# PEER's dense gates: one-hots in groups of two tokens instead of four, sixteen products at a time

## The chip, the cores and the metric

One core of a Trainium2 chip runs the whole program. Its engines work side by side and wait for one another through semaphores: TensorE (PE, matmuls; PEld, its weight loads), VectorE (DVE), ScalarE (ACT), GpSimd (POOL) and SyncE (SP, which issues most DMAs). The metric is the device time of one execution in microseconds; smaller is better.

## What is computed

The reference is two transformer layers one after the other, 512 tokens of 1024 channels: a hybrid layer with a mixture of 64 experts, then a mixer (attention and retention) with a PEER layer. The change is in PEER. Each token has 8 heads; each head finds the 16 best of 128 first and 128 second keys, and of their sums the 16 best, which name 16 of 128 x 128 = 16384 experts. An expert is one row of u and one of v:

```
    sc, ci = lax.top_k(cand, PEER_TOPK)
    eidx = (e1 * PEER_NKEYS + e2).reshape(T, PEER_HEADS * PEER_TOPK)
    gates = jax.nn.softmax(sc, axis=-1).reshape(T, PEER_HEADS * PEER_TOPK).astype(x.dtype)
    ...
        act = jax.nn.gelu(jnp.einsum('td,tkd->tk', xt, peer_u[it]), approximate=False)
        return jnp.einsum('tk,tkd->td', gt * act, peer_v[it])
```

## The kernel before

PEER handles 384 of the 512 tokens densely: all 16384 activations of each (products over u), times a dense table of gates that is zero but for the 128 picks of the token, and products over v. The last 128 tokens' picks are gathered row by row beside that.

**The turns over u.** `peer_u` runs 128 turns. In each, PE does 24 matmuls p_pu of 384 columns (eight k tiles, three passes of a float32 split into whi and wlo), ACT applies Gelu (pact, or a tile that stays on chip), and DVE makes the wlo of a later turn, after ACT's whi; every second turn SP loads 1 MB of u (raw, three tiles deep) and stores the activations (actd). Beside this DVE has a list `work` of steps with estimated costs, which are spread over 120 of the 128 turns (`PACE_U`): first the top-k steps, then the dense gates. After them in each turn stand the gathered picks (`peer_picks`, prow, line 1990). DVE's order is the order of the code; PE, ACT, POOL and SP are put into order by a scheduler that works with modelled times.

**The dense gates.** `peer_gates` (line 1943) makes the table of four tokens a call, 96 calls. The gate of (second key, first key) is a sum over the token's 128 picks, which lie on the partitions; so it is a matmul of two one-hot matrices [128 picks, 128 keys], one of them weighted by the gate. A gate is the sum of two float16, ghi and glo, so there are two matmuls for each token, 768 in all (lines 1961 and 1962, p_gt). The one-hots are built by DVE for eight tokens at once, at every second call: hot2 and hot1 by comparing iota4 with the keys' numbers e2T and e1T (line 1954), ghi and glo by multiplying hot1 (lines 1955 and 1956); four operations on [128, 2, 128, 4] float16, that is two groups with the four tokens of a group side by side for each key:

```
            four = lambda n: pk[n][:, 32 * c + 4 * j:32 * c + 4 * j + 8].rearrange("p (g t) -> p g t", t=4)[:, :, None, :].to_broadcast(
                [128, 2, 128, 4])
```

One token's matrix is therefore read with a step of 4 elements, as weights (hot2) and as moving columns (ghi, glo). The results of four tokens fill one PSUM bank p_gt (two of them), which ACT copies into gst (line 1963); after 32 tokens SP stores gst, 2 MB, to gd (line 1965). `peer_v` reads gd back when all is done.

Of the kernel before, what the change touches and what calls it, by code (L numbers as in the profile page):

```python
# [10 lines left out]
F32 = mybir.dt.float32  # L11
# [11 lines left out]
# steps of the retention's q and k per turn of the attention  # L23
ATTN_RATE = 2
EPS = 1e-6
# PEER: tokens on the dense path, tiles of their activations that stay on chip (some in x's place); the pace of the work beside the products
# over u, the turns between which the other tokens' picks are gathered, and how many gathers run ahead
ND, KEEP, KEEP_X, PACE_U = 384, 20, 8, 120
PICK_START, PICK_END, AHEAD = 8, 254, 4
# MoE: weight tiles beside those of the other phases  # L30
RAW2 = 6
X_LOAD = (3, 4, 5, 6)
# the experts before which the shared expert's steps are taken
SHARED, TURN, SHARED_DOWN = (12, 19, 26, 33), (37, 41), (45, 48, 51, 54)
# key tiles of the neighbourhood windows, in column-major tokens
# [3 lines left out]
# columns of the packed per-partition vectors: name -> (first column, count)  # L39
# [12 lines left out]
# rows that are spread over the partitions: name -> (first, count)  # L52
# [3 lines left out]
class K:  # L56
# [60 lines left out]
    def split_raw(self, t, n=2048, step=1024):  # L117
        """a list of (hi, lo) for each step columns of t"""
        out = []
        for o in range(0, n, step):  # L120
            m = min(step, n - o)
            hi = self.pair.tile([128, 1024], F32R, name="whi", tag="whi")
            lo = self.pair.tile([128, 1024], F32R, name="wlo", tag="wlo")
            self.split(hi[:, :m], lo[:, :m], t[:, o:o + m])
            out.append((hi, lo))
        return out

    def halves(self, load, n, ahead=2):
        """(hi, lo) of the n halves of the tiles load(i), split some turns before they are used"""
# [12 lines left out]
    def proj(self, out, w, act, nk, cols=slice(None), start=True, stop=True):  # L142
        """out[m, t] (+)= sum over k of w[k, m] act[k, t]; w holds nk tiles [128, 128]"""
# [5 lines left out]
    def rstd(self, pool, ps, src, nch, n, width, tag="mm", bufs=None):  # L149
        """[128, n] in PSUM: 1 / sqrt(mean over the channels of src^2 + eps), on every partition"""  # L150
        return self.rstd_end(pool, ps, self.rstd_sums(pool, ps, src, nch, n, tag, bufs), n, width, tag, bufs)
# [28 lines left out]
    def modulated(self, pool, src, rb, a, b, hi, lo, chunks, n):  # L180
        """(hi, lo) of src * a * rb + b by channel (a, b: columns)"""
# [7 lines left out]
    # ------------------------------------------------------------------ first block, up to the MoE  # L189
    def block1(self):  # L190
        nc, A = self.nc, self.A
        with ExitStack() as es:
# [4 lines left out]
            # the sums of the experts' results, in two parts, and 128 rows for the empty places  # L197
            self.yd = [d.tile([640, 1024], F32, name=f"yd{i}") for i in range(2)]
            self.dr = d = self.pool(es, "b1_dram", space=DRAM)
            # q, k of each head of the neighbourhood as [hi, lo, hi], [hi, hi, lo]: one product over them is the three  # L200
# [8 lines left out]
            # zeros, then the accumulator of the other modulation  # L209
# [29 lines left out]
    def mod_mix(self, ps, p, q, x):  # L239
        """the modulation's columns of sh_mix, sc_mix, for x and ctx; the latter as norm_mix_g (1 + sc). And the rstd of x."""  # L240
# [33 lines left out]
    def meta_norm(self, q):  # L274
        """the meta tokens' norm by g_mix"""
# [14 lines left out]
    def qkv(self, q, s, w, ctx, mod, hc):  # L290
# [22 lines left out]
        for g in range(7):  # L313
            if g:
                w = self.load_pair(A["w_qkv"][g])
            for j in range(2):
# [25 lines left out]
                elif t < 10:  # L342
                    if t == 8:
                        # there's time for it after this
# [14 lines left out]
        # v of the neighbourhood: tokens on partitions  # L359
# [12 lines left out]
    def tiny_qk(self, q, pt, pc, rope, perm):  # L372
# [5 lines left out]
        # the rotations' swapped halves, and k moved to the lower partitions  # L378
# [51 lines left out]
    def na(self):  # L430
        """the neighbourhood attention, four heads at a time, beside the products of the spatial gating's v"""
# [89 lines left out]
    def v_steps(self, q):  # L521
        """v, turned so that tokens are on partitions, in small steps"""
# [48 lines left out]
    def gating(self, es):  # L571
        """spatial gating: v mixed over the chunk, the tiny attention's output, times u"""
# [34 lines left out]
    def mod_rest(self, s):  # L607
        """the modulation's other columns (g_mix, sh_ffn, sc_ffn, g_ffn), a quarter in four steps:
        acc[d, i] += silu(c)[d] w_ada[d, i]; sc_ffn as norm_ffn_g (1 + sc)"""
# [69 lines left out]
    # ------------------------------------------------------------------ the MoE  # L679
    # Its input is (x a) rstd + b, by channels; products over x a need no rstd: it is a token's, and comes after them.  # L680
    def ffn_open(self):
# [3 lines left out]
        # the places, from 1 on, four times  # L685
# [9 lines left out]
        # a token's number + 1, its weight for an expert in three parts that add up to it  # L695
# [11 lines left out]
    def ffn_begin(self, q):  # L707
        """b and its products with the router, on every partition"""
# [3 lines left out]
        # x a, then the MoE's input, then x by tokens  # L712
# [22 lines left out]
    def row_of(self, out, m):  # L735
        """four columns of modf as a row, on every partition"""
# [4 lines left out]
    def ffn_chunk(self, S, m):  # L741
        """when 128 channels of x are final"""
# [7 lines left out]
        if m == 6:  # L750
            # the table of Sqrt is loaded ahead
# [72 lines left out]
    def route(self, q, S):  # L824
        """the tokens' rstd, the MoE input's rows in DRAM, from which the experts gather, and who gathers what"""
# [13 lines left out]
        # scores, the eight best, and their weights  # L839
# [23 lines left out]
        # a token's place in its expert's list, and the first two experts' tokens  # L863
# [6 lines left out]
        # places from 1 on, 0 for the tokens that aren't in the list  # L870
# [8 lines left out]
    def route_end(self):  # L879
        """the experts' weights, by token"""  # L880
# [13 lines left out]
    def parts(self, out, w, rest):  # L894
        """w as the sum of three fp16 in out's last dimension"""
# [6 lines left out]
    def hots(self, e, hots, out, cols):  # L902
        """out[i] = cols of the token at place i of expert e's list"""
# [4 lines left out]
    def slots(self, e0, n):  # L908
        """for n experts the tokens of their first 128 places, and their weights"""
# [16 lines left out]
    def blocks(self, q):  # L926
        """counts beyond 128: which expert each further block of 128 places belongs to, and its first place"""
# [15 lines left out]
        # experts all of whose further blocks come before block b  # L943
# [8 lines left out]
        # first place: 128 (1 + block - blocks of the experts before)  # L952
# [6 lines left out]
    def rows_of(self, q, v, g):  # L959
        """v: token + 1, or 0 in an empty place -> its row, or one beyond all tokens'"""  # L960
# [5 lines left out]
    def places(self, q, pt, g, w):  # L966
        """pt: (token + 1 or 0, its weight's parts) per place -> rows (of the last ones), weights"""
# [7 lines left out]
    def shared(self, step):  # L975
        """the shared expert's gates and ups, in four steps"""
# [12 lines left out]
    def by_tokens(self, m0):  # L989
        """512 channels of x, tokens on partitions"""  # L990
# [8 lines left out]
    def shared_down(self, step):  # L999
        """x += g_ffn * the shared expert, by tokens, in four steps"""  # L1000
# [19 lines left out]
    def expert_load(self, e):  # L1020
        """the weights of expert e (a number, or in a register): [gate | up] in two halves of its rows, down"""
# [17 lines left out]
    def expert_block(self, xg, gi, ws, w, yd):  # L1039
        """adds the rows' results times ws and g_ffn to yd; w: the expert's weights, or what loads them"""  # L1040
# [38 lines left out]
    def spare_places(self):  # L1079
        """the first block beyond an expert's first 128 places, if any"""  # L1080
# [11 lines left out]
    def overflow(self, n):  # L1092
        """the other such blocks, one at a time"""
# [14 lines left out]
    def further(self, c, gi, ws):  # L1108
        """the tokens, and their weights, of the 128 places of expert c[0] from place c[1] on"""
# [18 lines left out]
    def tail_loads(self):  # L1128
        """what the sum of the results and the next norm need"""
# [5 lines left out]
    def routed_first(self):  # L1135
        """the first accumulated results"""
# [11 lines left out]
    def load_after(self, src, x):  # L1148
        """src, loaded once x is there"""
# [5 lines left out]
    # ------------------------------------------------------------------ the second block's mixer  # L1155
    def mixer(self):
        with ExitStack() as es:
# [3 lines left out]
            # the tokens, then the meta tokens  # L1161
# [1090 lines left out]
```

## Time and profile before

| what | us |
|---|---|
| three runs, lowest, median, highest | 3225.7, 3234.66, 3238.91 |
| span of the profiled execution | 3229.2 |
| PE busy (share of the span) | 3114.6 (96%) |
| DVE busy | 2240.4 (69%) |
| ACT busy | 1390.3 (43%) |
| first product of the gates starts at | 2313.1 |
| last product of the gates starts at | 2644.3 |

The span runs from the first to the last instruction of the profiled execution; that execution's time is not listed apart from it, and the span lies within the times of the three runs. The gates' stretch is a tenth of the program. In the profile a line of a helper (102 for most matmuls, 105 and 106 for the split into whi and wlo) serves many tiles, so the tiles' names tell which product is meant; buffer numbers are left out, so hot stands for hot1 and hot2, and piota for iota4.

### The profile page before, as it was taken

What the parts mean: (1) busy time and instruction counts of PE and PEld (TensorE: products, weight loads), DVE (VectorE), ACT (ScalarE), POOL (GpSimd) and SP (SyncE); (2) the same over time, 40 slices, a digit from 0 to 9 for tenths busy, and PEclk for the clock granted to TensorE, in tenths of its full rate; (3) what the DMA queues carried; (4) which work ended last, traced back from release to release, by engine and by line L of the source; (5) the groups of instructions that cost most, each with busy time, mean ns of one, the idle gap of its engine ahead of it and who ended that gap; (6) DMA issues with size and microseconds to landing.
All of it is one profiled execution on the core that took longest, in us unless ns stands there. A gap on an engine that the chain in (4) does not pass through costs nothing.

```text
span 3229.2 us, 45060 instructions
## 1 busy us (share of the span) xinstructions
PE 3114.6 (96%) x16976; PEld 2613.2 (81%) x16976; DVE 2240.4 (69%) x4077; ACT 1390.3 (43%) x2195; POOL 567.2 (18%) x452
## 2 busy tenths in 40 slices
PE   8999999999999999799999999999999999999997
PEld 4877888666666666587877788999999999999997
DVE  7467744687767777657532336999977867888885
ACT  5356433454444544354454324444444433333332
POOL 0200000132223223200000000233422213222221
PEclk9999999899999999999999999999999999999999
DMA  6554645499999999831211223677888889999996
GB/s 245 173 173 137 229 152 205 145 371 324 355 332 334 359 355 346 260 134 66 77 68 50 80 97 119 222 272 272 274 311 287 296 288 335 348 342 347 344 343 195
DMA packets 236495, 779.99 MB, mean 242 GB/s; under 512 B 28773, under 2 KB 108133, under 8 KB 190453
## 3 DMA queue, kind: packets, MB, share of 16 engines
q1 hardware_dynamic: 167136, 570.88, 48.1%
q0 software_dynamic: 66368, 200.38, 20.7%
q10 hardware_dynamic: 2772, 5.85, 0.5%
q8 instruction: 134, 2.20, 0.3%
q14 instruction: 85, 0.69, 0.1%
HBM read 692.29 MB, written 101.97 MB: 246 GB/s over the span
## 4 chain that ended last, share of the span: by engine, by line
PE 80%; DVE 7%; issue 5%; DMA 4%; ACT 2%; POOL 0%; SPq 0%; POOLq 0%; DVEq 0%; ACTq 0%
PE p_y L102 16%; PE p_pu L102 11%; PE p_gu L102 10%; PE p_y L1072 6%; PE p_za L102 3%; PE p_ga L102 3%; PE p_z L102 2%; DVE wlo L106 2%; PE p_xt L1046 2%; PE p_all L1267 1%; PE p_gt L1961 1%; PE p_gt L1962 1%; PE p_rg L102 1%; PE p_out L102 1%; PE p_mx L102 1%
## 5 line engine op out<-in xcount | busy, mean ns | idle before, releaser
L105 ACT ACTIVATE whi<-raw 128x1024 fp32r<-128x1024 f32 (+1 forms) x686 | 711.4, 1049 | 1037.2 <-PE p_gu L102 241.4
L106 DVE TENSOR_TENSOR wlo<-raw,whi 128x1024 fp32r<-128x1024 f32 (+1 forms) x686 | 822.7, 1207 | 405.8 <-ACT whi L105 378.5
L102 PE MATMUL p_pu<-xp,whi 128*128 128x384 f32 x2048 | 533.6, 339 | 5.0 <-ACT pact L1836 4.8
L102 PEld LDWEIGHTS p_pu<-xp,whi 128*128 128x128 f32 x2048 | 370.0, 189 | 8.0 <-ACT pact L1836 7.6
L102 PE MATMUL p_gu<-whi,xt 128*128 128x512 f32 x1040 | 357.3, 412 | 0.2 <-ACT whi L105 0.2
L102 PE MATMUL p_pu<-xp,wlo 128*128 128x384 f32 x1024 | 347.8, 341 | 4.6 <-DVE wlo L106 4.4
L102 PE MATMUL p_y<-vlo,whi 128*128 128x384 f32 x1024 | 342.0, 334 | 0.0
L102 PE MATMUL p_y<-vhi,wlo 128*128 128x384 f32 x1024 | 342.0, 334 | 0.0
L102 PE MATMUL p_y<-vhi,whi 128*128 128x384 f32 x1024 | 287.7, 334 | 1.4 <-ACT pkept L1836 1.4
L1980 POOL DMA_INDIRECT prow<-in_pu_rows,rows x128 | 182.7, 1427 | 465.7 <-DVE prow L1990 425.5
L1072 PE MATMUL p_y<-raw,eat 128*128 128x512 f32 x520 | 236.4, 595 | 2.7 <-DVE eat L1066 1.5
L102 PEld LDWEIGHTS p_gu<-whi,xt 128*128 128x128 f32 x1040 | 197.5, 190 | 50.5 <-issue 11.2
L102 PE MATMUL p_gu<-wlo,xt 128*128 128x512 f32 x520 | 223.2, 429 | 4.9 <-DVE wlo L106 4.7
L1980 POOL DMA_INDIRECT prow<-in_pv_rows,rows x128 | 140.3, 1096 | 369.6 <-DVE yr L1996 356.4
L102 PEld LDWEIGHTS p_pu<-xp,wlo 128*128 128x128 f32 x1024 | 193.1, 189 | 10.0 <-DVE wlo L106 9.6
L102 PEld LDWEIGHTS p_y<-vhi,wlo 128*128 128x128 f32 x1024 | 192.2, 188 | 0.0
L102 PEld LDWEIGHTS p_y<-vlo,whi 128*128 128x128 f32 x1024 | 192.2, 188 | 0.0
L102 PEld LDWEIGHTS p_y<-vhi,whi 128*128 128x128 f32 x1024 | 187.3, 188 | 1.7 <-ACT pkept L1836 1.7
L1072 PEld LDWEIGHTS p_y<-raw,eat 128*128 128x128 f32 x520 | 97.5, 191 | 101.7 <-issue 89.6
L1076 POOL DMA_INDIRECT yd<-ey,gidx x64 | 116.2, 1816 | 282.5 <-DVE ey L1075 266.0
L1996 DVE SCALAR_TENSOR_TENSOR yr<-prow,pdots,yr 128x1024 f32<-128x1024 f32 x128 | 163.8, 1279 | 0.2
L1990 DVE SCALAR_TENSOR_TENSOR prow<-prow,xr 128x1024 f32<-128x1024 f32 x128 | 155.3, 1217 | 1.6 <-DMA prow<-in_pu_rows,rows 1.5
(704 smaller groups left out, 5658.0 us busy)
## 6 DMA issues: line engine op xcount, KB each, us to landing
raw<-in_w_moe SPq DMA_DIRECT2D x195, 1024.0 KB
raw<-in_pu SPq DMA_DIRECT2D x64, 1024.0 KB
raw<-in_pv_rows SPq DMA_DIRECT2D x64, 1024.0 KB
raw<-in_w_mod SPq DMA_DIRECT2D x24, 1024.0 KB
gd<-gst SPq DMA_DIRECT2D x12, 2048.0 KB
vgt<-gd SPq DMA_DIRECT2D x32, 768.0 KB
actd<-pact SPq DMA_DIRECT2D x54, 384.0 KB
vact<-actd SPq DMA_DIRECT2D x54, 384.0 KB
```

The costliest lines, as they stand in the source:

```text
L102: nc.tensor.matmul(out, a, b, start=start and i == 0, stop=stop and i == len(passes) - 1)
L105: self.nc.scalar.activation(hi, src, AF.Copy)
L106: (lo_engine or self.nc.vector).tensor_tensor(lo, src, hi.bitcast(F32), ALU.subtract)
L1046: nc.tensor.transpose(pt[:, 128 * k:128 * k + 128], xg[:, 512 * g + 128 * k:512 * g + 128 * k + 128], self.ident)
L1072: nc.tensor.matmul(py, at[:, 128 * k:128 * k + 128], wd[:, 1024 * k + 512 * n:1024 * k + 512 * n + 512], start=k == 0, stop=k == 1)
L1076: nc.gpsimd.indirect_dma_start(out=yd[:], out_offset=bass.IndirectOffsetOnAxis(ap=gi, axis=0), in_=y[:], in_offset=None, bounds_check=639, ...
L1267: self.nc.tensor.matmul(pts[i][:, :264], w[a][:, 128 * k:128 * k + 128], self.hn[b][:, k, 264 * i:264 * i + 264], start=k == 0 and n == 0, ...
L1961: nc.tensor.matmul(pt[:, i, :], hots["hot2"][:, j % 2, :, i], hots["ghi"][:, j % 2, :, i], start=True, stop=False)
L1962: nc.tensor.matmul(pt[:, i, :], hots["hot2"][:, j % 2, :, i], hots["glo"][:, j % 2, :, i], start=False, stop=True)
L1980: nc.gpsimd.indirect_dma_start(out=t[:], out_offset=None, in_=A["pu_rows" if i < 128 else "pv_rows"], in_offset=bass.IndirectOffsetOnAxis( ...
L1990: nc.vector.scalar_tensor_tensor(t, t, 1.0, self.xr, ALU.mult, ALU.mult, accum_out=dots[:, k:k + 1])
L1996: nc.vector.scalar_tensor_tensor(self.yr, t, dots[:, k:k + 1], self.yr, ALU.mult, ALU.add)
```

## The change

The one-hots are laid out [128, 4, 128, 2]: four groups of two tokens, so a token's matrix is read with a step of 2 elements; iota4 becomes iota2, half as long. A call of `peer_gates` now covers eight tokens (48 calls, at twice the estimated cost), builds the four one-hot tiles, and puts their sixteen matmuls, the two copies and, after the fourth call, the store of gst into a function. That function goes into `self.late` and runs in the next turn, after its p_pu and Gelu and ahead of that turn's steps for DVE. The opening of the pool for the products over v is put off in the same way.

```
-        self.iota4 = p.tile([128, 128, 4], F16, name="piota4")
+        self.iota2 = p.tile([128, 128, 2], F16, name="piota2")
...
         for c in range(ND // 32):
-            for j in range(8):
-                work.append((1.3, lambda c=c, j=j: self.peer_gates(self.pg, c, j)))
-        work.append((0.0, gates_done))
+            for j in range(4):
+                work.append((2.6, lambda c=c, j=j: self.peer_gates(self.pg, c, j)))
+        work.append((0.0, lambda: self.late.append(gates_done)))
...
                 nc.scalar.activation(act[:, j, :], pt[:, :ND], AF.Gelu)
+                late, self.late = self.late, []
+                for f in late:
+                    f()
                 while at < len(work) and done <= total * (2 * g + j + 1) / PACE_U:
...
-        if j % 2 == 0:
-            four = lambda n: pk[n][:, 32 * c + 4 * j:32 * c + 4 * j + 8].rearrange("p (g t) -> p g t", t=4)[:, :, None, :].to_broadcast(
-                [128, 2, 128, 4])
-            hots = {n: q.tile([128, 2, 128, 4], F16, name=n, tag=n) for n in ("hot2", "hot1", "ghi", "glo")}
...
+        two = lambda n: pk[n][:, 32 * c + 8 * j:32 * c + 8 * j + 8].rearrange("p (g t) -> p g t", t=2)[:, :, None, :].to_broadcast(
+            [128, 4, 128, 2])
+        hots = {n: q.tile([128, 4, 128, 2], F16, name=n, tag=n) for n in ("hot2", "hot1", "ghi", "glo")}
...
-        pt = ps.tile([128, 4, 128], F32, name="p_gt", tag="gt", bufs=2)
-        hots = self.gate_hots
-        for i in range(4):
-            nc.tensor.matmul(pt[:, i, :], hots["hot2"][:, j % 2, :, i], hots["ghi"][:, j % 2, :, i], start=True, stop=False)
-            nc.tensor.matmul(pt[:, i, :], hots["hot2"][:, j % 2, :, i], hots["glo"][:, j % 2, :, i], start=False, stop=True)
-        nc.scalar.activation(self.gst[:, :, 4 * j:4 * j + 4], pt.rearrange("p a b -> p b a"), AF.Copy, scale=2.0 ** -14)
-        if j == 7:
-            nc.sync.dma_start(self.gd[c], self.gst)
+        def products():
+            if j == 0:
+                self.gst = q.tile([128, 128, 32], F32, name="gst", tag="gst")
+            for o in (0, 4):
+                pt = ps.tile([128, 4, 128], F32, name="p_gt", tag="gt", bufs=2)
+                for i in range(4):
+                    g, t = divmod(o + i, 2)
+                    nc.tensor.matmul(pt[:, i, :], hots["hot2"][:, g, :, t], hots["ghi"][:, g, :, t], start=True, stop=False)
+                    nc.tensor.matmul(pt[:, i, :], hots["hot2"][:, g, :, t], hots["glo"][:, g, :, t], start=False, stop=True)
+                nc.scalar.activation(self.gst[:, :, 8 * j + o:8 * j + o + 4], pt.rearrange("p a b -> p b a"), AF.Copy, scale=2.0 ** -14)
+            if j == 3:
+                nc.sync.dma_start(self.gd[c], self.gst)
+        self.late.append(products)
```

On DVE the instructions stand in the same order as before. On PE the scheduler made other groups. First PE, in the middle of one block of eight tokens, near the middle of the gates' stretch, before: p_gt_22144 and p_gt_22189 are the PSUM tiles of its first and last four tokens, hot2_22136 its one-hots as weights, p_pu the products over u of the turn.

```order
L1961 LDWEIGHTS hot2_22136
L1961 MATMUL p_gt_22144<-ghi_22138,hot2_22136 128x128
L1962 LDWEIGHTS hot2_22136
L1962 MATMUL p_gt_22144<-glo_22139,hot2_22136 128x128
L102 MATMUL p_pu_22159<-xp0_16673,wlo_22041 128x384
L102 MATMUL p_pu_22159<-xp0_16673,whi_22040 128x384
L102 MATMUL p_pu_22159<-xp1_16674,whi_22040 128x384
L102 MATMUL p_pu_22159<-xp0_16673,wlo_22041 128x384
L1961 LDWEIGHTS hot2_22136
L1961 MATMUL p_gt_22189<-ghi_22138,hot2_22136 128x128
```

And at the same block now (lines 1971 and 1972 are the two matmuls; the tiles are p_gt_22179 and p_gt_22189):

```order
L1971 LDWEIGHTS hot2_22136
L1971 MATMUL p_gt_22179<-ghi_22138,hot2_22136 128x128
L1972 LDWEIGHTS hot2_22136
L1972 MATMUL p_gt_22179<-glo_22139,hot2_22136 128x128
L1971 LDWEIGHTS hot2_22136
L1971 MATMUL p_gt_22189<-ghi_22138,hot2_22136 128x128
```

Between the first and the last four tokens stood four p_pu; now the sixteen matmuls of a block stand in a row. Counted over the whole stretch, PE's order had 122 groups of p_gt between p_pu's, and has 63.

Second ACT, some 14 turns into the gates, before: whi is the split of the weights over u (its next instruction on DVE is wlo), pact the Gelu of a turn, gst the copy of four tokens' gates.

```order
L1963 ACTIVATE gst<-p_gt 128x128x4 x2
L105 ACTIVATE whi<-raw 128x1024
L1836 ACTIVATE pact<-p_pu 128x384
L1963 ACTIVATE gst<-p_gt 128x128x4
L105 ACTIVATE whi<-raw 128x1024
L1836 ACTIVATE pact<-p_pu 128x384
L1963 ACTIVATE gst<-p_gt 128x128x4 x2
```

And now, a few turns further on:

```order
L1973 ACTIVATE gst<-p_gt 128x128x4 x2
L105 ACTIVATE whi<-raw 128x1024
L1837 ACTIVATE pact<-p_pu 128x384
L105 ACTIVATE whi<-raw 128x1024
L1837 ACTIVATE pact<-p_pu 128x384
L1973 ACTIVATE gst<-p_gt 128x128x4 x2
```

The copies stood alone or in pairs, so that those of one block were spread over two turns; now they stand always in pairs, and about every fifth turn has none.

## Rows read from the trace of the kernel before

**Rows 1.** The page's slices, busy tenths of 40 equal slices of the span.
```profile
PE   8999999999999999799999999999999999999997
...
DMA  6554645499999999831211223677888889999996
```

**Rows 2.** Windows: length, PE, PEld, DVE, ACT, POOL busy, clock, DMA share, GB/s.
```profile
2313.00:2645.00 332.00, 332.00 (x2140) 313.07 (x2139) 258.15 (x371) 137.29 (x214) 75.92 (x62) 1.00 0.82 289
2700.00:3100.00 400.00, 400.00 (x2310) 400.00 (x2309) 327.39 (x389) 150.90 (x194) 107.84 (x100) 1.00 0.98 345
2050.00:2310.00 260.00, 249.61 (x1400) 241.32 (x1400) 251.42 (x897) 112.73 (x163) 98.79 (x60) 1.00 0.78 275
```

**Rows 3.** The chain of waits, 2313 to 2645 us, shares by line.
```profile
by line: PE p_pu L102 72.4%; PE p_gt L1961 13.8%; PE p_gt L1962 13.8%
```

**Rows 4.** Groups, 2313 to 2645 us: count | busy us, mean ns | idle before.
```profile
L102 PE MATMUL p_pu<-xp,whi 128*128 128x384 f32 x914 | 243.8, 344 | 0.0
...
L102 PE MATMUL p_pu<-xp,wlo 128*128 128x384 f32 x458 | 156.9, 343 | 0.0
L1961 PE MATMUL p_gt<-ghi,hot 128*128 128x128 f16 x384 | 97.6, 295 | 0.0
...
L106 DVE TENSOR_TENSOR wlo<-raw,whi 128x1024 fp32r<-128x1024 f32 x59 | 72.7, 1231 | 62.6 <-ACT whi L105 48.7 <-PE p_gt L1962 12.6 <-PE p_pu L102 1.2
L105 ACT ACTIVATE whi<-raw 128x1024 fp32r<-128x1024 f32 x58 | 61.6, 1062 | 68.0 <-PE p_pu L102 62.5 <-issue 5.1
L1963 ACT ACTIVATE gst<-p_gt 128x512 f32<-128x512 f32 x96 | 57.4, 597 | 127.3 <-PE p_gt L1962 126.8 <-issue 0.2
...
L1955 DVE TENSOR_TENSOR ghi<-hot,ghT 128x1024 f16<-128x1024 f16 x47 | 32.5, 692 | 1.6
...
L1954 DVE TENSOR_TENSOR hot<-piota,e1T 128x1024 f16<-128x1024 f16 x47 | 32.2, 684 | 0.0
```

**Rows 5.** Timeline of PE, the first burst: start us, length us, instruction.
```profile
2313.15 0.40 PE L1961 MATMUL p_gt<-ghi,hot 128*128 128x128 f16 x2
2313.37 0.30 PE L1962 MATMUL p_gt<-glo,hot 128*128 128x128 f16 x1
...
2314.91 0.29 PE L1962 MATMUL p_gt<-glo,hot 128*128 128x128 f16 x1
```

**Rows 6.** Timeline of PE, p_pu ahead of that burst.
```profile
2310.02 0.51 PE L102 MATMUL p_pu<-xp,whi 128*128 128x384 f32 x2
2310.37 0.33 PE L102 MATMUL p_pu<-xp,wlo 128*128 128x384 f32 x1
...
2312.62 0.51 PE L102 MATMUL p_pu<-xp,whi 128*128 128x384 f32 x2
```

**Rows 7.** Timeline of PE, a product alone between p_pu's.
```profile
2345.87 0.29 PE L1961 MATMUL p_gt<-ghi,hot 128*128 128x128 f16 x1
2345.93 0.42 PE L102 MATMUL p_pu<-xp,whi 128*128 128x384 f32 x1
2346.20 0.29 PE L1961 MATMUL p_gt<-ghi,hot 128*128 128x128 f16 x1
```

**Rows 8.** Timeline of PE, first block, matmuls of 512 columns.
```profile
59.82 0.39 PE L102 MATMUL p_in<-h,whi 128*128 128x512 f32 x1
...
63.67 0.61 PE L102 MATMUL p_in<-h,whi 128*128 128x512 f32 x2
```

**Rows 9.** Timeline of PE in the MoE: the experts' lists.
```profile
617.09 0.40 PE L906 MATMUL p_tb<-tk,hot 128*128 128x4 f16 x8
```

**Rows 10.** Line 906, the same matmuls: ns min/median/max.
```profile
L906 PE MATMUL p_tb<-tk,hot x256: 166/173/228, 614.5 to 1218.9; 128*128 128x4 f16 x128
```

**Rows 11.** Line 1381, kg by its norm: ns min/median/max.
```profile
L1381 DVE TENSOR_TENSOR kg<-kg,k_r x5: 662/680/692, 1442.5 to 1458.8; 128x512 f32<-128x512 f32 x4, 16x512 f32<-16x512 f32 x1
```

**Rows 12.** Line 1668, a product of two tiles: ns min/median/max.
```profile
L1668 DVE TENSOR_TENSOR z<-z,z x8: 691/692/694, 1790.0 to 1926.7; 128x512 f32<-128x512 f32 x8
```

More of the change, by code (lines that the diff above doesn't have):

```diff
@@ L1780, in peer_u @@
                 next(best, None)
-        nc.vector.tensor_copy(self.iota4, iota[:, :, None].to_broadcast([128, 128, 4]))
+        nc.vector.tensor_copy(self.iota2, iota[:, :, None].to_broadcast([128, 128, 2]))
         nc.vector.tensor_copy(self.codes[:, 1], iota[:, :16, None].to_broadcast([128, 16, 16]))
@@ L1825, in peer_u @@
         for c in range(ND // 32):
-            for j in range(8):
-                work.append((1.3, lambda c=c, j=j: self.peer_gates(self.pg, c, j)))
-        work.append((0.0, gates_done))
+            for j in range(4):
+                work.append((2.6, lambda c=c, j=j: self.peer_gates(self.pg, c, j)))
+        work.append((0.0, lambda: self.late.append(gates_done)))
         total, done, at = sum(w[0] for w in work), 0.0, 0
+        self.late = []
         for g in range(64):
@@ L1843, in peer_u @@
                 nc.sync.dma_start(self.actd[2 * g:2 * g + 2].rearrange("a p t -> p a t"), act)
-        while at < len(work):
-            work[at][1]()
-            at += 1
+        while at < len(work) or self.late:
+            late, self.late = self.late, []
+            for f in late:
+                f()
+            if at < len(work):
+                work[at][1]()
+                at += 1
     def peer_topk(self, q, qT, keys, t, h, S):
@@ L1946, in peer_gates @@
         nc, ps, pk = self.nc, self.ps, self.pk
-        if j == 0:
-            self.gst = q.tile([128, 128, 32], F32, name="gst", tag="gst")
-        if j % 2 == 0:
-            four = lambda n: pk[n][:, 32 * c + 4 * j:32 * c + 4 * j + 8].rearrange("p (g t) -> p g t", t=4)[:, :, None, :].to_broadcast(
-                [128, 2, 128, 4])
-            hots = {n: q.tile([128, 2, 128, 4], F16, name=n, tag=n) for n in ("hot2", "hot1", "ghi", "glo")}
-            for n, e in (("hot2", "e2T"), ("hot1", "e1T")):
-                nc.vector.tensor_tensor(hots[n], self.iota4[:, None].to_broadcast([128, 2, 128, 4]), four(e), ALU.is_equal)
-            nc.vector.tensor_tensor(hots["ghi"], hots["hot1"], four("ghT"), ALU.mult)
-            nc.vector.tensor_tensor(hots["glo"], hots["hot1"], four("glT"), ALU.mult)
-            self.gate_hots = hots
@@ L1964, in peer_gates @@
-        if j == 7:
-            nc.sync.dma_start(self.gd[c], self.gst)
+        two = lambda n: pk[n][:, 32 * c + 8 * j:32 * c + 8 * j + 8].rearrange("p (g t) -> p g t", t=2)[:, :, None, :].to_broadcast(
+            [128, 4, 128, 2])
+        hots = {n: q.tile([128, 4, 128, 2], F16, name=n, tag=n) for n in ("hot2", "hot1", "ghi", "glo")}
+        for n, e in (("hot2", "e2T"), ("hot1", "e1T")):
+            nc.vector.tensor_tensor(hots[n], self.iota2[:, None].to_broadcast([128, 4, 128, 2]), two(e), ALU.is_equal)
@@ new lines, in peer_gates @@
+        nc.vector.tensor_tensor(hots["ghi"], hots["hot1"], two("ghT"), ALU.mult)
+        nc.vector.tensor_tensor(hots["glo"], hots["hot1"], two("glT"), ALU.mult)
+        def products():
[10 more added lines that the diff above has]
+                nc.sync.dma_start(self.gd[c], self.gst)
```

## Prediction

> **What bounds the kernel now.** I read the 40 slices first: PE has 9 in nearly every one [rows 1], so time can only come out of what PE does, or out of what it waits for. Then the stages in which the changed code runs. [...] The chain of work that ended last runs through PE alone there: p_pu 72.4%, the gates' products p_gt 13.8% and 13.8% [rows 3]. So a microsecond of PE saved there is a microsecond of the kernel's time, until another engine takes over.
>
> The busy time of a group on PE can't be added up, since matmuls overlap (a p_gt is listed with 295 ns [rows 4]). The cost is the distance from one start to the next. In the first burst sixteen products start between 2313.15 and 2314.91, fifteen steps: 0.117 us each [rows 5]. The p_pu matmuls of 384 columns start every 2.60 / 15 = 0.1733 us, from the two at 2310.02 over five rounds of three to 2312.62 [rows 6]. Put together: 768 x 0.117 = 89.9 us for the products, 1372 (914 and 458) x 0.1733 = 237.8 us for p_pu [rows 4], and 4.3 us that are left over. The order in which PE gets its instructions has 122 groups of p_gt between p_pu's, so that is 0.035 us a group, and the trace shows it once by itself: from a lone p_gt at 2345.87 over one p_pu to the next p_gt at 2346.20 are 0.33 us, 0.04 more than 0.173 + 0.117 [rows 7].
>
> **The products, which decide.** Their number stays at 768, with the same 128 columns each; what changes is how far one column lies from the next. A column of hot2, ghi or glo was 4 float16 elements (8 bytes) behind the one before; now 2 (4 bytes). What does 0.117 us stand for? Two matmuls without gaps between columns give the price of a column: 384 columns take 0.1733 us [rows 6], 512 columns 3.85 / 17 = 0.2265 us, seventeen steps of p_in [rows 8]; the difference is 0.416 ns a column, and 0.0136 us are left as a fixed part. A product of 128 columns would take 128 x 0.416 ns + 0.0136 = 0.067 us at that price. At twice the price of a column it would take 0.120, and 0.117 is measured: the columns of the products come in at half rate.
>
> Are they slow for their distance, or because each needs a weight load of its own? The load by itself is cheap: in the MoE's lists the same kind of load (128 columns of float16, 8 bytes apart) with a matmul of 4 columns goes through eight times in 0.40 us [rows 9], of which the last takes 0.173 [rows 10], so (0.40 - 0.173) / 7, some 0.033 us a pair. So not the load, but the moving columns set 0.117. A column of the p_pu, which is float32, is 4 bytes long, so the next column lies 4 bytes on and passes at full rate; this is the distance that the change gives the float16 columns. No row shows float16 columns 4 bytes apart, so I bound the product: 0.053 us from below (full rate and no fixed part), 0.117 from above (nothing changes). I take 0.067, the price of the f32 rows with the same distance: 768 x (0.117 - 0.067) = **38.4 us** less, with a bound of 49.2 us the one way and nothing the other way.
>
> **The order on PE.** Sixteen products now stand together: 63 groups instead of 122. 59 x 0.035 to 0.04 = **2.1 to 2.4 us** less.
>
> **DVE.** Each eight tokens take four operations of 1024 float16 elements before and after, in the same places of DVE's order. They take 684 to 692 ns [rows 4], half of the 1231 ns of the float32 subtraction with as many elements [rows 4]: two elements at a time. The innermost run of each operand becomes 2 elements long, which is still a pair, so I cost it at nothing. The bound: if pairs are lost, 1.231 - 0.69 = 0.54 us for each of 192. Below nothing there is no reason, as the element count is the same. A one-element-wide repeat can be seen in the trace: one f32 word of r8 is read 64 times in a row by kg's product, which takes 680 ns [rows 11], while a product of 512 float32 elements without such a repeat takes 692 [rows 12]. A word read again costs nothing there. iota2 is written once, ahead of the stretch, and is half as long: nothing.
>
> **What else moves.** The products of a block are emitted after the next turn's p_pu, with their 96 copies gst (597 ns each [rows 4]) and the 12 stores gd. On PE the first burst stands at the same row as before; on ACT the copies stand in pairs behind pact, as they mostly did; behind a waiting copy the next whi is queued, and behind that wlo on DVE. That wait exists already: whi itself waits for p_pu for 62.5 us and the copies for p_gt 126.8 us [rows 4], all of it in the cover of a full PE; were PE not full, the copies' 57 us would count on an ACT that is busy 137 of 332 us [rows 2]. On SP two of the stores go out one weight load later, in a queue that loads three tiles ahead. POOL's gathers are where they were. All at nothing, as long as PE is the bound.
>
> **What is late next.** 332 - 38.4 - 2.2 = 291.4 us for the stretch. DVE's 258 us would be 89% of it; in the top-k stretch before it DVE is busy 251.4 of 260 us [rows 2], 97%. The DMA share would rise to 0.82 x 332 / 291.4 = 0.93 and 329 GB/s; in the stretch 2700 to 3100 PE is busy 400 of 400 us at a share of 0.98 and 345 GB/s [rows 2]. Neither takes over, but both come near, so I leave 1 us for friction.
>
> **Sum.** 38.4 + 2.2 - 1 = 39.6 us off the profiled span of 3229.2 us: 3189.6. The median of the runs lies 5.5 us above that span, at 3234.66, and I take the difference as it is: **3195 us**, 1.2% faster.
>
> **Rivals.**
> *Nothing changes on PE.* Float16 columns might pass at half rate whenever there is any gap between them, or the 0.117 us might have a cause that I don't see; 4 bytes then cost what 8 did, and only the 2 us of the order are gained: 3232.5 us. For it: no row has float16 columns side by side, so half rate is shown for float16 alone with a gap. Against it: the number falls on twice the price of a column, which the bytes explain. [...]
>
> *The load is laid bare.* At 0.067 us the stream might no longer cover the weight load; then a product takes 0.067 + 0.033 = 0.100 us, and 768 x 0.017 + 2.2 = 15.3 us are gained: 3220 us. Against it: 0.033 us fit twice into 0.067, and the loads of p_tb already run beside its matmuls.
>
> *Slower: DVE loses its pairs.* If runs of two elements make DVE take one element at a time, 192 operations cost 0.54 us more, 104 us; DVE has 258 + 104 = 362 us to do, at 97% in 373 us, 41 us over the 332: 3276 us. It decides from 332 x 0.97 - 258 = 64 us, so from 0.33 us more per operation; below that PE's gain shrinks. Against it: a run of two is a pair, and the repeated word costs nothing in [rows 11, 12]. [...]
>
> **How the numbers follow.** Chances: the forecast 0.67, nothing on PE 0.16, the bare load 0.09, DVE 0.08. The forecast by itself spans 3183 (0.053 us a product) to some 3206 (0.08 us). The range must take in the bare load and about half of the case in which PE gains nothing (3232.5, with the spread of the runs around it), so it ends at **3233**, and it begins at **3183**; DVE's case and the rest are left out. About 0.5% (16 us) is what a measurement of this kernel can tell from no change, so faster means below 3218.5: the forecast and half of the bare load, 0.72; same 0.20; slower 0.08.
>
> **What would show it.** In the profile after: p_gt starts 0.06 to 0.07 us apart inside a burst (0.117: first rival; 0.1: second); sixteen in a row; the stretch from the first to the last p_gt some 290 us with PE still full; the hot, ghi and glo operations at 0.68 to 0.70 us (1.0 or more: third rival); DVE busy near 258 us and the DMA share near 0.93. The prediction is wrong if PE shows idle time in the stretch, waiting for wlo or for raw: then DVE or the DMA has taken over and part of the 38 us is given back; or if the later stretch 2700 to 3100 gets longer, which nothing here touches.

## The result and the profile after

The changed kernel takes 3192.05 us (median of four runs, 3188.55 to 3200.51), the kernel before 3236.78 beside it (3225.7 to 3239.02): a ratio of 0.987, with a 95% interval of 0.9855 to 0.9882. The prediction was 3195 us.

The windows of the kernel after (length, PE, PEld, DVE, ACT, POOL busy, granted clock, DMA share, GB/s; the first from the first to the last product of the gates):

```profile
2322.00:2608.00 286.00, 286.00 (x2136) 276.84 (x2135) 254.96 (x370) 130.09 (x212) 90.78 (x62) 1.00 0.91 333
...
2700.00:3100.00 400.00, 400.00 (x2309) 400.00 (x2308) 327.06 (x388) 149.66 (x192) 109.51 (x100) 1.00 0.98 344
```

These answer to the first two of [rows 2]. The stretch of the gates is 286 us long; it was 331.2, from 2313.1 to 2644.3. PE is still busy all through, at the same clock, DVE has the same work (255 us, now 89%), and the DMA share rose from 0.82 to 0.91. The later stretch of 400 us is as it was. So 45.2 us went out of one stretch, on the engine that bounds it. The profiled span is only 36.4 us shorter (3192.8 after 3229.2), because in this execution the products over u began 9 us later (2024.6, before 2015.7). That lies ahead of everything that changed and differs from run to run: in a second profile of the same kernel (`after_again`, below) they began at 2019.0 and the span was 3187.4; the gates' stretch was 286.0 us there too. From the last p_pu to the end both kernels take 551.7 us (from 2677.5 before, from 2641.1 after).

The chain of waits in that stretch, against [rows 3], and the timeline of PE in one block of sixteen products and behind it (start us, length us, instruction), against [rows 5]:

```profile
by line: PE p_pu L102 84.3%; PE p_gt L1971 8.0%; PE p_gt L1972 7.8%
```

```profile
2327.82 0.22 PE L1972 MATMUL p_gt<-glo,hot 128*128 128x128 f16 x1
2327.88 0.22 PE L1971 MATMUL p_gt<-ghi,hot 128*128 128x128 f16 x1
2327.94 0.22 PE L1972 MATMUL p_gt<-glo,hot 128*128 128x128 f16 x1
2328.00 0.22 PE L1971 MATMUL p_gt<-ghi,hot 128*128 128x128 f16 x1
...
2328.51 0.22 PE L1971 MATMUL p_gt<-ghi,hot 128*128 128x128 f16 x1
2328.57 0.22 PE L1972 MATMUL p_gt<-glo,hot 128*128 128x128 f16 x1
2328.59 0.42 PE L102 MATMUL p_pu<-xp,wlo 128*128 128x384 f32 x1
2328.85 0.52 PE L102 MATMUL p_pu<-xp,whi 128*128 128x384 f32 x2
```

From 2327.82 to 2328.57 are thirteen steps: 0.0577 us from one product to the next, where [rows 5] had 0.117. (The block's first product stands apart, one p_pu ahead, at 2327.45. 37 of the 48 blocks have all sixteen in a row; in the other eleven, the second to the twelfth, one or two stand apart, hence 63 groups and not 48.) The groups of the same stretch, against [rows 4] (count | busy us, mean ns of one | idle before):

```profile
L102 PE MATMUL p_pu<-xp,whi 128*128 128x384 f32 x912 | 241.4, 339 | 0.0
...
L106 DVE TENSOR_TENSOR wlo<-raw,whi 128x1024 fp32r<-128x1024 f32 x58 | 71.2, 1227 | 22.8 <-ACT whi L105 22.8
L105 ACT ACTIVATE whi<-raw 128x1024 fp32r<-128x1024 f32 x58 | 61.6, 1062 | 144.9 <-PE p_pu L102 132.6 <-issue 12.3
L1971 PE MATMUL p_gt<-ghi,hot 128*128 128x128 f16 x384 | 52.2, 221 | 0.0
L1973 ACT ACTIVATE gst<-p_gt 128x512 f32<-128x512 f32 x94 | 50.7, 595 | 12.2 <-PE p_gt L1972 12.2
...
L1971 PEld LDWEIGHTS <-hot 128*128 128x128 f16 x384 | 36.2, 97 | 8.6 <-issue 6.4 <-DVE glo L1962 1.3 <-DVE hot L1960 0.3
L1961 DVE TENSOR_TENSOR ghi<-hot,ghT 128x1024 f16<-128x1024 f16 x47 | 32.5, 692 | 1.6
...
L1960 DVE TENSOR_TENSOR hot<-piota,e1T 128x1024 f16<-128x1024 f16 x47 | 32.1, 683 | 0.0
```

DVE's four operations take 683 to 692 ns, as before to within a nanosecond or two. ACT's idle time moved to another name: the copies gst used to wait for p_gt (126.8 us) and now mostly find it done (12.2), and whi waits for p_pu in their place (132.6 us, it was 62.5). In all ACT is idle for 156 of 286 us, where it was 195 of 332. Nothing of that reaches PE, which has no idle time in this stretch.

### The profile page after: what moved, and what is told of

Read it like the earlier page. It is cut to its first block, busy times and chain, and to the rows that moved or that the text cites. A ratio compares the mean times of both kernels' runs of the same rounds, so it can differ in the third digit from the quotient of the medians.

```text
span 3192.8 us, 45059 instructions
## 1 busy us (share of the span) xinstructions
PE 3071.1 (96%) x16976; PEld 2576.9 (81%) x16976; DVE 2237.8 (70%) x4077; ACT 1384.8 (43%) x2195; POOL 584.6 (18%) x452
## 4 chain that ended last, share of the span: by engine, by line
PE 46%; DVE 5%; issue 4%; ACT 1%; DMA 1%; POOL 0%; POOLq 0%; ACTq 0%; DVEq 0%
PE p_y L102 17%; PE p_pu L102 11%; PE p_za L102 3%; PE p_z L102 2%; PE p_all L1267 1%; PE p_rg L102 1%; PE p_yr L102 1%; PE p_mx L102 1%; DVE wlo L106 1%; DVE prow L2002 1%; PE r_s L1614 1%; PE r_y L1624 1%; PE p_ya L102 1%; PE p_gt L1971 1%; PE p_gt L1972 1%
## 5 line engine op out<-in xcount | busy, mean ns | idle before, releaser
L1992 POOL DMA_INDIRECT prow<-in_pu_rows,rows x128 | 197.6, 1544 | 405.4 <-DVE prow L2002 365.4
## 6 DMA issues: line engine op xcount, KB each, us to landing
raw<-in_w_moe SPq DMA_DIRECT2D x195, 1024.0 KB, 12.2
```

The source lines that it names most:

```text
L1992: nc.gpsimd.indirect_dma_start(out=t[:], out_offset=None, in_=A["pu_rows" if i < 128 else "pv_rows"], in_offset=bass.IndirectOffsetOnAxis( ...
```

## Experiments

Two things came closer by the change, PE's weights (hot2) and its moving columns (ghi, glo), and two things were done together, the layout and the order. The first four kernels take them apart.

**Moving columns left at four tokens** (in the edits W is the number of tokens in a group of the weights, M in a group of the moving columns).

```
-        hots = {n: q.tile([128, 4, 128, 2], F16, name=n, tag=n) for n in ("hot2", "hot1", "ghi", "glo")}
...
+        W, M = 2, 4
+        of = {"hot2": W, "hot1": M, "ghi": M, "glo": M}
...
+        hots = {n: q.tile([128, 8 // g, 128, g], F16, name=n, tag=n) for n, g in of.items()}
```

> hot2 (the weights of the products over the gates) in groups of two, hot1, ghi and glo (the moving columns) in groups of four; everything else as after. Theory M, the distance between the moving columns sets the rate: products start 0.117 to 0.118 us apart as before, the stretch of the products takes about 331 us, the time is 3233 to 3238 us. Rival W, the weight load sets the rate: 0.057 us apart, stretch 286 us, 3190 to 3194 us. Rival H, each of the two gives half: 0.087 us apart, 3212 to 3217 us.

Measured: 3232.43 us, ratio 0.999 (0.998 to 0.9999). The windows from the first to the last product, and the timeline of PE in one group:

```profile
2321.80:2650.20 328.40, 328.40 (x2136) 319.07 (x2136) 257.06 (x370) 136.53 (x213) 77.99 (x62) 1.00 0.83 292
```

```profile
2328.39 0.30 PE L1977 MATMUL p_gt<-glo,hot 128*128 128x128 f16 x1
2328.51 0.30 PE L1976 MATMUL p_gt<-ghi,hot 128*128 128x128 f16 x1
2328.63 0.30 PE L1977 MATMUL p_gt<-glo,hot 128*128 128x128 f16 x1
2328.75 0.30 PE L1976 MATMUL p_gt<-ghi,hot 128*128 128x128 f16 x1
2328.87 0.30 PE L1977 MATMUL p_gt<-glo,hot 128*128 128x128 f16 x1
```

0.117 to 0.12 us from product to product, with weights as close as after. Theory M holds, W and H fall. The stretch is 328.4 us, a little shorter than the 331 that M gave.

**The reverse: weights left at four tokens.**

```
+        W, M = 4, 2
+        of = {"hot2": W, "hot1": M, "ghi": M, "glo": M}
```

> The reverse: hot2 in groups of four, hot1, ghi and glo in groups of two. Theory M: 0.057 us apart, stretch about 286 us, 3190 to 3194 us. Rival W: 0.117 us apart, stretch 331 us, 3233 to 3238 us. Rival H: 0.087 us, 3212 to 3217 us.

Measured: 3192.54 us, ratio 0.9873 (0.9856 to 0.989).

```profile
2317.10:2605.90 288.80, 288.80 (x2136) 279.69 (x2135) 255.23 (x370) 130.44 (x212) 91.72 (x62) 1.00 0.90 330
```

All but 2.8 us of the stretch's gain is there with the moving columns alone. How the loads of hot2 are recorded doesn't tell what closer weights are worth: 114 to 116 ns here and 97 after, but 113 to 115 in `w2m4` too, where the weights are as close as after and only the products are slow. Groups from 2325 to 2600 us, `w4m2` first:

```profile
L1976 PEld LDWEIGHTS <-hot 128*128 128x128 f16 x355 | 39.5, 114 | 8.0 <-issue 6.6 <-DVE glo L1967 0.5 <-DVE hot L1965 0.5
```

```profile
L1976 PEld LDWEIGHTS <-hot 128*128 128x128 f16 x312 | 35.0, 113 | 7.2 <-issue 5.0 <-DVE prow L2007 0.8 <-DVE ghi L1966 0.6
```

The stretches do tell it: closer weights bring 2.8 us beside products of 0.058 us, and 1.8 beside those of 0.117 (330.2 in the next kernel, 328.4 in `w2m4`).

**The order without the layout** (the same edit, with groups of four for both):

```
+        W, M = 4, 4
```

> All four one-hots in groups of four as before, but built for eight tokens and their sixteen products emitted together one block later, as after. Theory M (the layout gives the gain, the order nothing): products 0.117 us apart, 3233 to 3238 us. The prediction's own term for the order alone (59 fewer groups at 0.035 to 0.04 us): 3234 to 3235 us, hardly told apart from it. Rival (the longer groups let weight loads hide): under 3215 us with products closer than 0.09 us.

Measured: 3233.67 us, ratio 0.9995 (0.9986 to 1.0005). The products start 0.118 us apart (median), so the longer groups by themselves don't make them faster.

**The layout without the order** (the loop and calls of before, with groups of two):

```
-            four = lambda n: pk[n][:, 32 * c + 4 * j:32 * c + 4 * j + 8].rearrange("p (g t) -> p g t", t=4)[:, :, None, :].to_broadcast(
-                [128, 2, 128, 4])
...
+            four = lambda n: pk[n][:, 32 * c + 4 * j:32 * c + 4 * j + 8].rearrange("p (g t) -> p g t", t=2)[:, :, None, :].to_broadcast(
+                [128, 4, 128, 2])
...
+            g, t = divmod(4 * (j % 2) + i, 2)
```

> Groups of two, but emitted as before: eight products at a time, in two turns, right where the one-hots are built. Theory M with a price at each way out of a group (0.061 us after products of 0.057 us, where the next float32 weight load is not covered, against 122 ways out instead of 62): products 0.057 us apart, stretch 3 to 5 us longer than after's 286 us, 3195 to 3197 us. If the way out costs nothing: 3191 to 3193 us. Rival (the short products need the long groups or the block's delay): over 3203 us, with idle PE or spacings over 0.07 us in the stretch.

Measured: 3195.7 us, ratio 0.9877 (0.9861 to 0.9894). The windows of the two, from the first to the last product, the order alone first:

```profile
2313.80:2644.00 330.20, 330.20 (x2136) 319.82 (x2136) 257.32 (x371) 136.76 (x213) 78.03 (x62) 1.00 0.83 291
```

```profile
2318.20:2608.50 290.30, 290.30 (x2135) 272.61 (x2134) 255.38 (x370) 131.77 (x212) 87.88 (x62) 1.00 0.89 327
```

So the stretch of 331.2 us loses 1.0 us by the order alone, 40.9 by the layout alone, and 45.2 by both. The order (longer groups, one turn later; the two were not tried apart) is worth 1.0 us with products of 0.117 us and 4.3 with products of 0.058. The timeline of the changed kernel above shows where that comes from. Behind the last product of a group, at 2328.57, the next p_pu starts at 2328.59 and the one after it only at 2328.85: 0.28 us from the last product to the second p_pu, where 0.0577 + 0.173 = 0.231 would be the pace of the two kinds. By the medians over the whole stretch a way out of a group costs 0.053 us and a way in 0.020 more than that pace, 0.073 a group; before, it was 0.014 for a group of several products. Multiplied by the 122 groups of `two_old` that is 8.9 us, by the 63 of after 4.6; their stretches have 9.1 and 4.9 us left over when products and p_pu are taken off. The float32 weight load of the first p_pu (188 ns in the records) used to have a product of 0.117 us ahead of it and now has one of 0.058; that this is the cause fits the numbers and was not tried by itself.

**Moving columns 16 bytes apart**, one group of eight, weights as after:

```
+        hots.update({n: q.tile([128, 128, 8], F16, name=n, tag=n) for n in ("hot1", "ghi", "glo")})
```

> hot2 in groups of two as after; hot1, ghi and glo in one group of eight, so that the moving columns lie 16 bytes apart. Law P, the time of a column goes with its distance beyond 4 bytes: 0.21 to 0.235 us a product, the stretch 403 to 422 us, the time 3309 to 3330 us. Law S, there are two rates, one up to 4 bytes and half of it beyond: 0.117 us, the time of w2m4, 3230 to 3238 us.

Measured: 3360.84 us, ratio 1.0385 (1.0365 to 1.0405). Windows of the whole stretch, then of five pieces in it (group of products, p_pu, group, p_pu, group), and the timeline of PE in one group:

```profile
2318.50:2773.00 454.50, 454.50 (x2136) 365.88 (x2135) 260.92 (x373) 140.31 (x213) 74.19 (x62) 0.90 0.61 212
```

```profile
2329.50:2331.70 2.20, 2.20 (x11) 1.11 (x10) 0.00 (x0) 0.60 (x1) 0.00 (x0) 1.00 0.85 314
2331.80:2335.90 4.10, 4.10 (x25) 3.98 (x23) 3.69 (x7) 0.69 (x2) 0.00 (x0) 1.00 0.82 288
2336.00:2339.60 3.60, 3.60 (x18) 1.85 (x18) 3.36 (x4) 1.85 (x3) 2.84 (x2) 1.00 0.28 59
2339.70:2342.90 3.20, 3.20 (x12) 3.18 (x11) 2.84 (x5) 0.60 (x1) 0.52 (x1) 0.53 0.74 255
2343.40:2346.50 3.10, 3.10 (x19) 2.46 (x18) 0.56 (x3) 1.26 (x2) 0.99 (x1) 1.00 0.24 48
```

```profile
2328.97 0.41 PE L1975 MATMUL p_gt<-ghi,hot 128*128 128x128 f16 x1
2329.20 0.41 PE L1976 MATMUL p_gt<-glo,hot 128*128 128x128 f16 x1
2329.43 0.41 PE L1975 MATMUL p_gt<-ghi,hot 128*128 128x128 f16 x1
2329.66 0.41 PE L1976 MATMUL p_gt<-glo,hot 128*128 128x128 f16 x1
```

0.229 us a product: law P, not S. The time is 31 us above the upper end that law P gave, and the clock explains it. After some of these groups the granted clock falls: 0.53 from 2339.7 to 2342.9, with 12 matmuls in 3.2 us where the piece from 2331.8 has 25 in 4.1. The products take 768 x (0.229 - 0.0577) = 131.6 of the 168.5 us by which the stretch is longer than after's; the p_pu that follow one another, 1254 of them, start 0.205 us apart in the mean instead of 0.1735, which is 40 us; together that is 172.

**Columns side by side**, groups of one, weights and moving columns:

```
+        W, M = 1, 1
```

> All four one-hots in groups of one: the columns of a token lie side by side (2 bytes apart), for PE's weights and moving columns alike; for VectorE the picks' operand repeats one value along the row instead of running over a pair. The prediction's slower rival, priced: if VectorE needs 1.22 us for each of the four operations in place of 0.684 to 0.692, its work in the stretch goes from 255 to about 358 us and bounds it, 3262 to 3275 us. If only the comparisons slow down: 3205 to 3220 us. If none does: 3190 to 3194 us. On PE, by both laws of the distance a product stays at 0.0535 to 0.0575 us; were the time of a column in proportion to its distance down to 2 bytes, 0.03 us.

Measured: 3265.73 us, ratio 1.0095 (1.0075 to 1.0114). The windows of the stretch, the groups of DVE's operations, what PE waited for (us in total, times, longest), and the timeline of PE in one group:

```profile
2317.80:2672.80 355.00, 311.03 (x2160) 283.82 (x2160) 352.34 (x369) 130.49 (x215) 102.75 (x60) 1.00 0.72 266
```

```profile
L1964 DVE TENSOR_TENSOR ghi<-hot,ghT 128x1024 f16<-128x1024 f16 x47 | 57.6, 1225 | 1.6
L1963 DVE TENSOR_TENSOR hot<-piota,e2T 128x1024 f16<-128x1024 f16 x47 | 57.3, 1220 | 0.0
```

```profile
PE p_pu L102 <- DVE wlo L106: 29.8, 35, 1.8
PE p_gt L1975 <- DVE glo L1965: 10.2, 24, 0.5
```

```profile
2330.73 0.22 PE L1974 MATMUL p_gt<-ghi,hot 128*128 128x128 f16 x1
2330.79 0.22 PE L1975 MATMUL p_gt<-glo,hot 128*128 128x128 f16 x1
2330.84 0.22 PE L1974 MATMUL p_gt<-ghi,hot 128*128 128x128 f16 x1
2330.90 0.22 PE L1975 MATMUL p_gt<-glo,hot 128*128 128x128 f16 x1
```

The slower rival is real, one step further on. With one token to a group DVE needs 1.22 us for each operation in place of 0.69, is busy 352 of 355 us, and PE waits for wlo and glo. PE itself gets next to nothing for it: 0.056 us a product, after 0.057 (medians). Of the groups of one, two and four, two is the one in which both engines keep their best rate (with four a product takes 0.117 us, and DVE's operations are at 684 to 692 ns as with two).

**One operation more for DVE** (ghi made twice):

```
         nc.vector.tensor_tensor(hots["ghi"], hots["hot1"], two("ghT"), ALU.mult)
+        nc.vector.tensor_tensor(hots["ghi"], hots["hot1"], two("ghT"), ALU.mult)
```

> After, with the operation that makes ghi issued twice: 48 more operations of VectorE of 0.692 us, 33.2 us in the stretch, where VectorE then has 288 us of work. Theory, VectorE has the room that the busy time shows (255 of 286 us) and no more: the stretch goes to 288 to 296 us, PE waits for wlo, the time is 3194 to 3203 us. Rival, the split tiles ahead cover it: 3190 to 3194 us. Rival, VectorE is already the bound in places: the whole 33 us, 3222 to 3226 us.

Measured: 3208.36 us, ratio 0.9921 (0.9903 to 0.9938).

```profile
2316.00:2620.00 304.00, 296.04 (x2161) 282.06 (x2158) 288.40 (x421) 130.37 (x214) 104.90 (x63) 1.00 0.85 314
```

33 us of work made the kernel 16 us slower, between the theory (at most 11) and the rival (all 33); so of the 31 us that DVE's busy time leaves free after the change some 17 were to be had. DVE is busy 288 of 304 us there, 95%. Of the 15.6 us in which it is not, 9.5 are two waits in its own queue, for a small step of the gathered picks (pdots) on ACT; what PE is listed as waiting for is mostly ACT's Gelu (pact), and wlo for only 1.3 us, where the theory had wlo. The group of DVE and the wait of PE behind these numbers:

```profile
L2007 DVE TENSOR_TENSOR pdots<-pdots,pgate 128x32 f32<-128x32 f32 x2 | 0.4, 194 | 9.5 <-ACT pdots L2006 9.5
```

```profile
PE p_pu L102 <- ACT pact L1837: 4.5, 11, 0.4
```

How DVE's load reaches PE by way of ACT was not taken apart. The stretch also holds 25 p_pu more than after's (4.3 us), so 304 less 286 overstates what it lost.

**A slower pace of all the work beside the products** (124 turns):

```
-ND, KEEP, KEEP_X, PACE_U = 384, 20, 8, 120
+ND, KEEP, KEEP_X, PACE_U = 384, 20, 8, 124
```

> After, with the pace of the work beside the products over u at 124 blocks in place of 120, so that the search for the best keys, beside which PE idles 10 us in 260, is spread over some 3.3% more blocks (8.6 us more room for VectorE). Theory, VectorE's total work bounds that stretch: 4 to 9 us faster than after, 3183 to 3188 us. Rival, the waits come from single bursts of work and stay: 3190 to 3194 us. Rival, the gates come too late for the first products over v: over 3196 us.

Measured: 3191.6 us (3185.76 to 3195.12), ratio 0.9865 (0.9844 to 0.9886): no difference from after that these runs can tell. What PE waited for there:

```profile
PE p_y L102 <- ACT vhi L2052: 5.7, 1, 5.7
```

Up to the first gate PE idles 8.5 us instead of 11.0, but the first product over v then waits 5.7 us in one piece, which after doesn't. What is won at one end is lost at the other.

**The pace of the gates alone.** The extra operation says that the gates' stretch has room, the windows say that the search for the best keys ahead of it has none (in `after` DVE is busy 251.2 of the 260 us from 2059 on, and PE 249.6). So the gates get fewer turns and the search more, with the same end:

```
-                work.append((2.6, lambda c=c, j=j: self.peer_gates(self.pg, c, j)))
+                work.append((2.3, lambda c=c, j=j: self.peer_gates(self.pg, c, j)))
```

> After, with a step of the gates at 2.3 in place of 2.6 in the plan of the work beside the products over u: the search for the best keys is then given about 64 of 120 blocks in place of 60, the gates 56 in place of 60, and the end stays where it is. A block adds some 1.6 us of room where VectorE bounds (4.16 us of PE, 2.3 to 2.6 us of VectorE), and takes the same from the gates' stretch, where 31 us of 286 are free. Theory: PE's idle time before the gates goes from 11.0 to about 4.5 us and the gates' stretch stays bound by PE: 3184 to 3188 us. Rival, the room of the gates' stretch is used up earlier than its busy share says (as with one more operation): the gain is given back there, 3190 to 3196 us.

> The same with 2.0: 68 blocks for the search, 52 for the gates, where VectorE then has about 91% to do. Theory: idle before the gates under 1 us, 3180 to 3185 us. Rival, VectorE bounds the gates' stretch: PE idles 5 us or more there, 3188 to 3196 us.

> The changed kernel as it is, beside the two others on the same chip: 3189 to 3195 us, the first products over u between 2016 and 2025 us and PE idle 10 to 11 us between there and the first gate.

Measured on one chip: 3185.88 us (3179.85 to 3189.08) with 2.3, 3184.09 (3181.41 to 3184.65) with 2.0, 3188.81 (3185.7 to 3192.0) for the changed kernel. Both changed paces lie within what their theory said. Windows from the first p_pu to the first gate and on to the last one, of `after_again` and of `gates20`:

```profile
2019.00:2316.50 297.50, 286.52 (x1598) 275.96 (x1596) 286.30 (x1043) 132.49 (x190) 101.01 (x62) 1.00 0.74 257
2316.50:2602.50 286.00, 286.00 (x2138) 276.90 (x2136) 254.97 (x370) 130.04 (x212) 90.58 (x62) 1.00 0.92 333
```

```profile
2022.10:2341.80 319.70, 316.17 (x1791) 309.93 (x1790) 304.32 (x1066) 144.80 (x207) 113.76 (x70) 1.00 0.78 271
2341.80:2597.10 255.30, 255.30 (x1948) 243.03 (x1948) 238.23 (x346) 120.59 (x196) 89.95 (x53) 1.00 0.91 336
```

PE's idle time ahead of the gates goes from 11.0 to 3.5 us with 2.0 and to 8.0 with 2.3, less of a gain than expected (under 1 and 4.5), and in the gates' stretch PE stays full with DVE at 93%. With 2.0 the way from the first to the last p_pu is 9.3 us shorter, but only 4.7 arrive in the span, and as many in the median: in these two profiles the first p_pu starts 3.1 us later with 2.0, and behind the last one 1.5 us are lost. The ranges of 2.0 and of the changed kernel don't touch, but the intervals of their ratios to before do (0.9819 to 0.9848, and 0.9835 to 0.9866), so this gain of 0.15% is likely rather than settled. Against the kernel before, 2.0 has 0.9834.

## Why the prediction was right, and where its terms were off

**What bounds the kernel** was read rightly: 45 us came off PE in the one stretch that was changed, where PE was 100% busy [rows 2], and the time followed. No other engine took over.

**The products.** The cause was right, and the reading that set the weight load aside too: moving columns 4 bytes apart in place of 8 give the gain without closer weights (`w4m2`), and closer weights without them don't (`w2m4`). The size was low. The term was 768 x (0.117 - 0.067) = 38.4 us; a product takes 0.0577, so it is 768 x 0.0593 = 45.5. The step that failed is the fixed part of 0.0136 us, taken from float32 matmuls of 384 and 512 columns: 128 x 0.416 ns are 0.0532 us, and only 0.0045 come on top. The lower bound, 0.053, was nearer.

**The order.** The term, 59 groups at 0.035 to 0.04 us, missed in both directions. By itself the order brings 1.0 us, since its price per group was taken as the stretch's whole remainder divided by the groups, and the p_pu that follow one another hold part of that (174.4 ns in the mean, where 173.3 were taken off). Together with fast products it brings 4.3, since beside these a way in or out is dearer; the layout alone pays for that, with 40.9 us in place of the 45.5 of its products. What is left over beside products and p_pu therefore stayed where it was, 4.3 us before and 4.9 after, with half the groups. So the sum's products were 7.1 us too low and its order 2.5 too high, and the stretch lost 45.2 us in place of 40.6.

**Why 3195 was still close.** Between the medians of the runs made beside each other the gain is 44.7 us, 5.1 more than the forecast's 39.6. That the time itself lies only 3 us from the forecast is in part luck: the median before was 2.1 us higher in these runs than the one that the forecast was counted from, and the two misses above partly cancel. The friction of 1 us isn't seen.

**The rivals.** Nothing on PE: excluded by 0.0577 us. A gap between float16 columns doesn't halve the rate by itself: 4 bytes apart a product takes 0.058 us, beside 0.056 with the columns side by side; 8 bytes apart takes 0.117 us, twice the 0.058 of 4, and 16 bytes 0.229. The bare load: not inside a group, where a product takes 0.058 us with a load of its own; what may be left of it is the 0.053 us at the way out of each. DVE's pairs: kept with two tokens, 683 to 692 ns. With runs of one float16 the loss is there, 1.22 us, and the time of 3265.7 us lies near the 3276 that the rival named.

**What is late next**: DVE and DMA stayed behind PE, as said, at 89% and 0.91. But the room behind DVE's 89% was smaller than it looks, as the extra operation showed. No one share marks the limit: PE was still full at DVE's 93% (gates at 2.0), was not at 95% (one operation more), and with one token to a group DVE itself reached 352 of 355 us, where the prediction's rival had it stop at 97%.

## What to carry to other kernels

Where PE streams operands of 2 bytes with a step, look at the distance in bytes from one moving column to the next, and lay the data out so that it is 4 bytes or less: beyond that the product's time goes with the distance (with 128 columns 0.056 us at 2 bytes and 0.058 at 4, but 0.117 at 8 and 0.229 at 16), while the weights' distance hardly counts here (1.8 to 2.8 us in 768 products). This was tried with float16 alone; whether bytes or elements set the rate of a wider type with a step, no run shows. The layout that PE wants and the one that DVE wants pull against each other (PE is as fast with one token as with two, 0.056 and 0.058 us a product; DVE needs two, for 0.69 us an operation in place of 1.22), so take the smallest group that DVE writes at full rate. And a price that was read beside slow instructions, such as that of breaking up a group (for a group of several products 0.014 us before, where they take 0.117 us, and 0.073 after, where they take 0.058), has to be read again once they are fast.

## What the runs showed that was not expected

A float16 product of 128 moving columns takes 0.056, 0.058, 0.117 and 0.229 us with the columns 2, 4, 8 and 16 bytes apart: flat up to 4 bytes, then in proportion. With 16 bytes the granted clock falls to 0.53 for stretches of some 3 us behind groups of these slow products, though PE is listed as busy throughout (454.5 of 454.5 us), and the p_pu behind pay for it with 0.32 us each in place of 0.173; the products' own pace stays at 0.229. With 8 bytes the clock stayed at 1.00. And weights 8 bytes apart in place of 4 cost the stretch 2.8 us in 768 products of 0.058 us, and 1.8 in products of 0.117; the recorded length of a load follows the products beside it as much as its own step (with close weights 113 to 115 ns beside products of 0.117 us, 97 beside those of 0.058).
